# The modulation sums of a two-layer backbone move from SBUF to a PSUM bank, its background loads are issued ahead of the stores, and its buffers move down by 32 bytes

## The chip, the cores and the metric

The kernel runs on one core of a Trainium2 chip. The metric is the device time of one execution in microseconds (us), the median of several runs. Everything is float32 in memory. In the text PE is the matrix engine (TensorE), DVE the vector engine, ACT the scalar engine, POOL the GpSimd engine and SP the engine that issues most of the DMAs.

## The reference, cut to what matters

The program has two layers over 1024 tokens of width 1024, with 256 context tokens. Layer 1 is windowed attention with 16 query heads, 4 key/value heads, head size 128, a sink logit and rotary positions. Layer 2 is a gated convolution block. Each layer is modulated by a vector made from `c`:

```python
for i in range(DEPTH):
    shift, scale, gate = jnp.split((silu_c @ ada_w[i] + ada_b[i])[:, None, :], 3, axis=-1)
    h_lat = modulate(rmsnorm(x, norm_g[i]), shift, scale)        # h * (1 + scale) + shift
    ...
    if kind == 0:
        y, y_ctx = attention_layer(h_lat, h_ctx, attn_w_in[j], attn_sink[j], attn_w_out[j], cos, sin, ctx_out)
    else:
        y = conformer_conv_branch(h_lat, conv_w_in[j], conv_b_in[j], conv_dw_w[j], ..., conv_w_out[j])
    x = x + gate * y
return rmsnorm(x, final_g)
```

In the attention, 128 queries of a head meet 256 context keys and up to 384 neighbours in one softmax (`sink_softmax`), and the output is multiplied by a gate path before `attn_w_out`.

## The kernel before, in words

**Products.** Each float32 product is made of three matmuls on a rounded part and a rest: hi x hi, hi x lo, lo x hi (`mm3`). A matrix is split by ACT, which writes the rounded part, and by a subtraction `split_lo` on DVE or POOL, which writes the rest. Weights of the projections are streamed by `WStream`: `load` fetches a chunk of 1024 x 128 numbers into a page (`wraw_page`), `split` makes `whi_page` on ACT and `wlo_page` on DVE or POOL.

**Memory.** One pool of 45 pages of 4 KB per partition and one of 6 half pages hold nearly all data. `alloc` takes the page that was freed longest ago, so a load into a page waits for the last reader that this page had. Smaller named tiles (`ctile`) lie in front of the pages, among them `ident`, `vt` and `sel` in this order. PSUM has the tiles `pss` (two of two banks), `psg` (two banks) and `pso` (the banks `o0` and `o1`, which `ps_o()` takes in turn).

**Stages.** Of the span, the first 100 us load inputs, make the first modulation and project keys, values and the first queries. From 100 to about 858 us runs the attention: 128 steps, one for each head and block of 128 queries. A step emits scores (`pss<-kh_page,qh_page` and its like), then `FILL` = 12 groups of background projection matmuls (`psg<-hh_page,whi_page`), then the transposes of the probabilities (`pss<-ident,p_page`), and after each fourth step the product with the values (`pv`, into a `pso` tile, evacuated by DVE as `oz_half<-pso,zs_page`). Beside PE, DVE makes the masked scores and their sum (`p_page<-pss,mask_page,nsink`, the sum in `sc`), ACT the exponentials, POOL the scaling `p_page<-p_page,sc`; ACT and DVE split the transposed probabilities into `pthi` and `ptlo`. At each fourth head (three times) a regroup projects the next key and value heads, emits `pv` and the first scores of the new group, and then turns the value block with four transposes in `vt_split` (`pso<-ident,vf_half`). From 858 to 1047 us follows the output projection, to 1500 us the input projection and convolution of layer 2, and then its norm and output projection.

**Background work of the attention.** Two generators are advanced by the steps. `ada_rest` makes the modulation that is still missing, the gate of layer 1 and all of layer 2: 16 groups of 256 columns, each the sum over 8 row blocks of `ada_w` (loaded in turn into the tiles `dww_raw` and `wsum_raw`) times the vector `cs`. The sum is kept in the last 256 columns of `mask_page` (`acc_a`): one `tensor_scalar`, two additions of the bias over `ident`, seven `scalar_tensor_tensor` (stt). One step later PE sums over the partitions with `ones`. `low_parts` prepares the rests of both output weights, 32 items of 512 KB: load into a `low_page`, ACT rounds a half (`lhi_half`), POOL subtracts, and the page is stored to `wolA` or `wolC` in DRAM. An item takes three steps; after heads 3, 7, 11 and 15 have passed their first `LOWS` = 5 steps, no new one is begun.

**Order.** PE's instructions keep the order of the program (`pin("P")`). The order on the other engines is set by a scheduler that works on estimated times. Each engine then runs its own list strictly in order, so an instruction that waits holds all behind it; this goes for SP too, where a load whose page is not free or a store whose data is not ready holds every later DMA.

Of the kernel before, what the change touches and what calls it, by code (L numbers as in the profile page):

```python
# [9 lines left out]
F32 = mybir.dt.float32  # L10
F32R = mybir.dt.float32r
AF = mybir.ActivationFunctionType
ALU = mybir.AluOpType
# [81 lines left out]
def backbone_kernel(  # L95
# [32 lines left out]
    def ps_o(i=None):  # L128
        if i is None:
            oflip[0] ^= 1  # L130
            i = oflip[0]
        return ps.tile([P, 512], F32, tag=f"o{i}", name=nm("pso"), bufs=1)
# [10 lines left out]
    def ctile(shape, dt, name):  # L143
        return cpool.tile(shape, dt, tag=name, name=name, bufs=1)
# [13 lines left out]
    def split_lo(eng, lo, full, hi):  # L158
        return tt(eng, lo, full, hi.bitcast(F32), ALU.subtract)

    ident = ctile([P, P], F32, "ident")
    vt = ctile([P, P], F32, "vt")
    sel = ctile([P, 2], F32, "sel")
    sink = ctile([P, NH], F32, "sink")
    nsink = ctile([P, NH], F32, "nsink")
    ones = ctile([P, P], F32, "ones")
# [34 lines left out]
    class WStream:  # L201
# [19 lines left out]
        def split(self, between=None):  # L221
            if self.ns >= self.nl:
                return
            i = self.ns
            r = self.raw.pop(i)
            h, l = pg.alloc(F32R, [KT, P], "whi"), pg.alloc(F32R, [KT, P], "wlo")
            if self.hp:
                with tc.high_priority():
                    act(h, r, AF.Copy)
                    split_lo(self.lo_eng(i), l, r, h)  # L230
            else:
                act(h, r, AF.Copy)
                if between:
                    between()
                split_lo(self.lo_eng(i), l, r, h)
            pg.free(r)
            self.hl[i] = (h, l)
            self.ns += 1
# [269 lines left out]
    for pr in range(NPR):  # L508
# [35 lines left out]
        if pr == 2:  # L544
# [2 lines left out]
            SY.dma_start(out=cos, in_=k_cos)  # L547
            SY.dma_start(out=sin, in_=k_sin)

    def vt_split(vf, n, dh, dl):  # L550

        tp = ps_o()
        for i in range(n // P):
            PE.transpose(tp[:, i * P:(i + 1) * P], vf[:, i * P:(i + 1) * P], ident)
        t3 = tp[:, 0:n].rearrange("p (a b) -> p a b", b=P)
        act(dh, t3, AF.Copy)
        split_lo(V, dl, t3, dh)
# [24 lines left out]
    def ada_rest():  # L582
        todo = [(l, c0) for l, c0 in [(0, 2048 + 256 * i) for i in range(4)] + [(1, 256 * i) for i in range(12)]]
        todo = [(l, c0, kt) for l, c0 in todo for kt in range(KT)]

        def load(i):
            l, c0, kt = todo[i]
            SY.dma_start(out=ada_raw[i % 2], in_=ada_w[l, kt * P:(kt + 1) * P, c0:c0 + 256])

        load(0)  # L590
        for i, (l, c0, kt) in enumerate(todo):
            if i + 1 < len(todo):
                load(i + 1)
            raw = ada_raw[i % 2]
            if kt == 0:
                after(V.tensor_scalar(out=acc_a, in0=raw, scalar1=cs[:, kt:kt + 1], scalar2=None, op0=ALU.mult))
                for b in range(2):
                    col = (c0 - 2048 if l == 0 else 1024 + c0) // P + b
                    bs = slice(b * P, b * P + P)
                    stt(acc_a[:, bs], ident, abt[:, col:col + 1], acc_a[:, bs], ALU.mult, ALU.add)  # L600
            else:
                after(stt(acc_a, raw, cs[:, kt:kt + 1], acc_a, ALU.mult, ALU.add))
            yield
            if kt < KT - 1:
                continue
            yield
            o = ps_o()
            if c0 >= 2048:
                PE.matmul(o[0:1, 0:256], ones[:, 0:1], acc_a, start=True, stop=True)
                V.tensor_copy(acc_a[0:1], o[0:1, 0:256])  # L610
                SY.dma_start(out=gd[l][:, c0 - 2048:c0 - 1792], in_=acc_a[0:1])
            else:
                for b in range(2):
                    PE.matmul(o[:, b:b + 1], acc_a[:, b * P:b * P + P], ones[:, 0:1], start=True, stop=True)
                V.tensor_copy(mod1[:, c0 // P:c0 // P + 2], o[:, 0:2])
# [9 lines left out]
    def pair_rows(ap, m, kk):  # L625

        return ap[kk * 256:kk * 256 + 256, m * 512:m * 512 + 512].rearrange("(a p) n -> p a n", p=P)

    def low_parts():

        items = [(pair_rows(w, m, kk), d[m, kk]) for w, d in ((Wo, wolA), (Wp, wolC)) for m in range(2) for kk in range(NK)]
        for src, dst in items:
            raw = pg.alloc(F32, [2, 512], "low")
            SY.dma_start(out=raw, in_=src)
            yield "open"
            for b in range(2):
                hi = hp.alloc(F32R, None, "lhi")
                act(hi[:, 0:512], raw[:, b], AF.Copy)
                after(split_lo(G, raw[:, b], raw[:, b], hi[:, 0:512]), anchor_p)
                hp.free(hi)  # L640
                if b == 0:
                    yield "open"
            SY.dma_start(out=dst, in_=raw)
            pg.free(raw)
            yield "shut"

# [313 lines left out]
    def enqueue(key):  # L962
        fillq.append((key, job(key)))
# [58 lines left out]
    def pv(h, half):  # L1022
        g = h // 4
        c, vh, vl = kvt[g][2:5]
        o = ps_o()
        q0 = half * 4
        work = [(*(c[:, n, i * P:i * P + P] for n in (2, 3)), slice(13 + 4 * i, 17 + 4 * i), slice(0, 512)) for i in range(2)]
        for kb in range(max(q0 - 1, 0), min(q0 + 4, TB - 1) + 1):
            qa, qz = max(kb - 1, q0), min(kb + 1, q0 + 3)
            b0 = 1 + 4 * (1 - (kb - qa)) + (qa - q0)  # L1030
            n = qz - qa + 1
            if n == 1 and kb > qa:
                work.append((vh[:, kb], vl[:, kb], slice(0, 5, 4), slice(256, 512)))
            elif n == 1:
                work.append((vh[:, kb], vl[:, kb], slice(9, 22, 12), slice(0, 256)))
            else:
                work.append((vh[:, kb], vl[:, kb], slice(b0, b0 + 5 * (n - 1) + 1, 5),
                             slice((qa - q0) * P, (qz - q0 + 1) * P)))
        for n, (a, b, ps_, os_) in enumerate(work):
            last = n == len(work) - 1  # L1040
            PE.matmul(o[:, os_], a, pthi[:, ps_], start=n == 0, stop=False)
            PE.matmul(o[:, os_], a, ptlo[:, ps_], start=False, stop=False)
            PE.matmul(o[:, os_], b, pthi[:, ps_], start=False, stop=last)
        sl = slice(half * 512, half * 512 + 512)
        oz = hp.alloc(F32, None, "oz")
        stt(oz[:, 0:512], o, 0.5, zt[h][:, sl], ALU.mult, ALU.mult)
        SY.dma_start(out=ozd[h, :, sl], in_=oz[:, 0:512])
        hp.free(oz)
        if half:
            pg.free(zt.pop(h))  # L1050
            pg.free(*qt.pop(h))
# [49 lines left out]
    lows = low_parts()  # L1101
    lstate = ["shut"]
    pvq = deque()
    enqueue(("z", 0))
    enqueue(("q", 1))
    fill(18)
# [4 lines left out]
    for i, (h, qb) in enumerate(steps):  # L1111
        if qb == 0:
            for n in (() if h % 4 == 3 else (h + 1,) if h % 4 or not h else (h, h + 1)):
                enqueue(("z", n))
                if n + 1 < NH:
                    enqueue(("q", n + 1))
        if (h, qb) == (NH - 1, EARLY_FROM - 2):
            run(lows)
        if h == NH - 1 and EARLY_FROM - 2 <= qb < EARLY_FROM:
            next(projA)  # L1120
        if (h, qb) == (NH - 1, EARLY_FROM):
            next(projA)
            fillq.append((("wo", 0), early_proj()))
        if lstate[0] == "open" or h and (h % 4 < 3 or qb < LOWS):
            lstate[0] = next(lows, "shut")
        nxt = steps[i + 1] if i + 1 < len(steps) else None
        regroup = nxt and nxt[1] == 0 and nxt[0] % 4 == 0
        if nxt and nxt[1] == 0:
            fill(1000, ("q", h + 1))
        if nxt and not regroup:  # L1130
            scores(*nxt)
        if not regroup:
            fill(15 if h and h % 4 == 0 and qb < 4 else FILL)
        if pvq:
            pv(*pvq.popleft())
        if regroup:
            g = nxt[0] // 4
            old = kvt[g - 1]
            run(job(("k", g)))
            transposes(h, qb)  # L1140
            run(job(("v", g)))
            pv(h, 1)
            pg.free(*old)
            scores(*nxt)
            vlate.pop(g)()
            continue
        transposes(h, qb)
        if qb % 4 == 3:
            pvq.append((h, qb // 4))
        for _ in range(2 if qb == 1 or qb == 6 and h % 2 else 1):  # L1150
            next(adag, None)
# [575 lines left out]
```

## Time and the profile before

| | before |
|---|---|
| runs | 1756.67, 1757.55, 1760.27 us |
| median | 1757.55 us |
| span of the profiled execution | 1752.9 us |
| PE busy / DVE / ACT / POOL | 98% / 66% / 51% / 51% |

For the profiled execution the span is known, not its own device time; the median of the runs stands 4.65 us above this span. A prediction of the time is made as the change of the span, added to the median. A row of a timeline gives the start, the duration, the engine, the operation with output and inputs, and in brackets how long the engine had been idle before it and what ended this idle time.

### The profile page before, as it was taken

What the parts mean: (1) busy time and instruction counts of PE and PEld (TensorE: products, weight loads), DVE (VectorE), ACT (ScalarE), POOL (GpSimd) and SP (SyncE); (2) the same over time, 40 slices, a digit from 0 to 9 for tenths busy, and PEclk for the clock granted to TensorE, in tenths of its full rate; (3) what the DMA queues carried; (4) which work ended last, traced back from release to release, by engine and by line L of the source; (5) the groups of instructions that cost most, each with busy time, mean ns of one, the idle gap of its engine ahead of it and who ended that gap; (6) DMA issues with size and microseconds to landing.
All of it is one profiled execution on the core that took longest, in us unless ns stands there. A gap on an engine that the chain in (4) does not pass through costs nothing.

```text
span 1752.9 us, 23877 instructions
## 1 busy us (share of the span) xinstructions
PE 1720.7 (98%) x8420; PEld 1424.8 (81%) x8420; DVE 1148.3 (66%) x2079; ACT 889.4 (51%) x1548; POOL 895.4 (51%) x705
## 2 busy tenths in 40 slices
PE   7999999999999999999999999999999999999997
PEld 4788888888888888888888888888888888788886
DVE  6755564556546563656315189999999999867823
ACT  7555553445345444545334355554665564466731
POOL 0245654566636565653101267998898888130300
PEclk9999999999999999999999999999999999999999
DMA  9334443444334542436777733011121202377971
GB/s 313 107 82 139 136 133 85 145 147 145 100 105 143 152 142 87 136 119 203 279 250 239 241 90 105 13 54 31 43 79 36 91 30 79 120 254 243 325 264 48
DMA packets 195324, 242.45 MB, mean 138 GB/s; under 512 B 11798, under 2 KB 126790, under 8 KB 195204
## 3 DMA queue, kind: packets, MB, share of 16 engines
q1 hardware_dynamic: 188516, 230.10, 40.3%
q10 hardware_dynamic: 6688, 10.83, 2.6%
q8 instruction: 66, 1.08, 0.3%
q14 instruction: 54, 0.44, 0.1%
HBM read 188.70 MB, written 41.69 MB: 131 GB/s over the span
## 4 chain that ended last, share of the span: by engine, by line
PE 86%; DMA 5%; DVE 3%; POOL 2%; ACT 2%; issue 2%; SPq 1%; ACTq 0%; POOLq 0%; DVEq 0%
PE psg L89 44%; PE pss L89 22%; PE pso L89 19%; DMA araw_page<-in_ada_w_dram 1%; POOL rope_half L89 1%; DMA low_page<-in_conv_w_out_dram 1%; DMA rope_half<-rope_half 1%; SPq L89 1%; DMA low_page<-in_attn_w_out_dram 1%; DMA wolC<-low_page 1%; DVE mask_page L89 1%; ACT p_page L89 0%; POOL wlo_page L89 0%; POOL low_page L89 0%; DMA wraw_page<-in_attn_w_in_dram 0%
## 5 line engine op out<-in xcount | busy, mean ns | idle before, releaser
L89 POOL TENSOR_TENSOR odd_half<-odd_half,prod_half 128x513 f32<-128x513 f32 (+2 forms) x252 | 312.8, 1250 | 24.2 <-ACT prod_half L89 11.0
L89 PE MATMUL psg<-hh_page,whi_page 128*128 128x512 f32 x600 | 237.6, 396 | 0.0
L89 PE MATMUL psg<-hh_page,wlo_page 128*128 128x512 f32 x600 | 236.9, 395 | 0.0
L89 PE MATMUL psg<-hl_page,whi_page 128*128 128x512 f32 x600 | 236.8, 395 | 0.0
L89 POOL TENSOR_TENSOR wlo_page<-wraw_page,whi_page 128x1024 fp32r<-128x1024 f32 x70 | 173.1, 2475 | 104.1 <-ACT whi_page L89 83.2
L89 ACT ACTIVATE prod_half<-ubuf,dww 128x513 f32<-128x513 f32 (+2 forms) x252 | 165.1, 674 | 107.3 <-POOL odd_half L89 105.1
L89 POOL TENSOR_SCALAR p_page<-p_page,sc 128x640 f32<-128x640 f32 (+1 forms) x128 | 100.8, 787 | 224.4 <-DVE sc L89 208.7
L89 PE MATMUL psg<-h2h_page,whi_page 128*128 128x512 f32 x464 | 183.9, 396 | 0.0
L89 PE MATMUL psg<-h2h_page,wlo_page 128*128 128x512 f32 x464 | 183.0, 394 | 0.0
L89 PE MATMUL psg<-h2l_page,whi_page 128*128 128x512 f32 x464 | 182.4, 393 | 0.0
L89 DVE SCALAR_TENSOR_TENSOR pss<-ubuf,dww,pss 128x512 f32<-128x512 f32 (+3 forms) x270 | 172.3, 670 | 0.1
L89 DVE SCALAR_TENSOR_TENSOR pss<-ubuf,wsum,pss 128x512 f32<-128x512 f32 (+3 forms) x270 | 171.7, 670 | 0.2
L89 DVE TENSOR_TENSOR ptlo<-pss,pthi 128x640 fp32r<-128x640 f32 (+1 forms) x144 | 103.3, 717 | 64.0 <-ACT pthi L89 62.8
L89 ACT ACTIVATE p_page<-p_page,sc 128x641 f32<-128x641 f32 (+1 forms) x128 | 102.7, 802 | 74.1 <-DVE sc L89 69.7
L89 ACT ACTIVATE pthi<-pss 128x640 fp32r<-128x640 f32 (+1 forms) x144 | 88.6, 615 | 91.7 <-PE pss L89 86.3
L89 PEld LDWEIGHTS psg<-hh_page,wlo_page 128*128 128x128 f32 x600 | 112.9, 188 | 26.3
L89 PEld LDWEIGHTS psg<-hh_page,whi_page 128*128 128x128 f32 x600 | 113.0, 188 | 20.8 <-DVE kvc_page L89 0.2
L89 PEld LDWEIGHTS psg<-hl_page,whi_page 128*128 128x128 f32 x600 | 112.9, 188 | 20.7
L89 ACT ACTIVATE whi_page<-wraw_page 128x1024 fp32r<-128x1024 f32 x88 | 92.6, 1053 | 69.0 <-PE psg L89 25.5
L89 PE MATMUL pso<-h2l_page,whi_page 128*128 128x512 f32 x304 | 119.9, 394 | 0.0
L89 PE MATMUL pso<-h2h_page,whi_page 128*128 128x512 f32 x304 | 119.8, 394 | 0.0
L89 PE MATMUL pso<-h2h_page,wlo_page 128*128 128x512 f32 x304 | 119.6, 394 | 0.0
(244 smaller groups left out, 4105.2 us busy)
## 6 DMA issues: line engine op xcount, KB each, us to landing
wraw_page<-in_conv_w_in_dram SPq DMA_DIRECT2D x48, 512.0 KB
wraw_page<-in_attn_w_in_dram SPq DMA_DIRECT2D x40, 512.0 KB
wol_page<-wolA SPq DMA_DIRECT2D x32, 512.0 KB
wo_page<-in_attn_w_out_dram SPq DMA_DIRECT2D x32, 512.0 KB
wo_page<-in_conv_w_out_dram SPq DMA_DIRECT2D x32, 512.0 KB
wol_page<-wolC SPq DMA_DIRECT2D x32, 512.0 KB
rope_half<-rope_half ACTq DMA_DIRECT2D x80, 128.0 KB
araw_page<-in_ada_w_dram SPq DMA_DIRECT2D x32, 256.0 KB
```

The lines of the kernel that those rows point to most:

```text
L89: r = f(*a, **k)
```

## The change

Five edits are made together.

1. The tile `sel` is dropped and its two columns become columns 112 and 113 of `vt`. Every tile and page behind it starts 32 bytes lower: before at 32 beyond a multiple of 64, now at a multiple of 64. `ident` and `vt` stay where they were.
2. Where POOL makes a `wlo_page`, it does so in two halves of 128 x 512 instead of one operation of 128 x 1024.
3. `ada_rest` keeps its sum in the left half of the PSUM bank `o1` for the whole attention. Sixteen copies of 128 x 256 from PSUM to `acc_a` are added, one step after the last product of a group; PE's sum over the partitions goes into the right half of the same bank.
4. As `o1` is taken, `pv` and `vt_split` use bank `o0` only during the attention.
5. The store of a low item is written behind the load of the next one, and its page is freed that much later. Where a step begins no item, the outstanding store is written at once.

```diff
-    sel = ctile([P, 2], F32, "sel")
+    sel = vt[:, 112:114]
 ...
-                split_lo(self.lo_eng(i), l, r, h)
+                if self.lo_eng(i) is G:
+                    for a in range(0, KT, KT // 2):
+                        split_lo(G, *(t[:, a:a + KT // 2] for t in (l, r, h)))
+                else:
+                    split_lo(self.lo_eng(i), l, r, h)
 ...
+    vbank = []
     def vt_split(vf, n, dh, dl):
-        tp = ps_o()
+        tp = ps_o(*vbank)
 ...
         load(0)
+        bank = ps_o(1)
+        acc, o = bank[:, 0:256], bank[:, 256:512]
 ...
-                after(V.tensor_scalar(out=acc_a, in0=raw, scalar1=cs[:, kt:kt + 1], scalar2=None, op0=ALU.mult))
+                after(V.tensor_scalar(out=acc, in0=raw, scalar1=cs[:, kt:kt + 1], scalar2=None, op0=ALU.mult))
 ...
-                    stt(acc_a[:, bs], ident, abt[:, col:col + 1], acc_a[:, bs], ALU.mult, ALU.add)
+                    stt(acc[:, bs], ident, abt[:, col:col + 1], acc[:, bs], ALU.mult, ALU.add)
             else:
-                after(stt(acc_a, raw, cs[:, kt:kt + 1], acc_a, ALU.mult, ALU.add))
+                after(stt(acc, raw, cs[:, kt:kt + 1], acc, ALU.mult, ALU.add))
             yield
             if kt < KT - 1:
                 continue
+            V.tensor_copy(acc_a, acc)
             yield
-            o = ps_o()
 ...
+    made = []
+    def store():
+        while made:
+            dst, raw = made.pop()
+            SY.dma_start(out=dst, in_=raw)
+            pg.free(raw)
     def low_parts():
         for src, dst in items:
             raw = pg.alloc(F32, [2, 512], "low")
             SY.dma_start(out=raw, in_=src)
+            store()
             yield "open"
 ...
-            SY.dma_start(out=dst, in_=raw)
-            pg.free(raw)
+            made.append((dst, raw))
             yield "shut"
+        store()
 ...
     def pv(h, half):
-        o = ps_o()
+        o = ps_o(0)
 ...
+    vbank.append(0)
     enqueue(("z", 0))
 ...
         if lstate[0] == "open" or h and (h % 4 < 3 or qb < LOWS):
             lstate[0] = next(lows, "shut")
+        else:
+            store()
```

PE's order is the same as before. The first place where another engine's order differs is on POOL, ahead of the first regroup (about 262 to 277 us of the span). Here `wlo` is the rest of a weight chunk, the two `rope` rows with the same number form the rotated query, and `ql` is its rest. Before:

```order
99 L89 TENSOR_TENSOR ql_page_2391<-rope_half_2480,qh_page_2390 128x512
100 L89 TENSOR_SCALAR p_page_2536<-p_page_2536,sc_2537 128x640
101 L89 TENSOR_TENSOR wlo_page_2643<-wraw_page_2277,whi_page_2642 128x1024
102 L89 TENSOR_SCALAR p_page_2578<-p_page_2578,sc_2579 128x512
103 L89 TENSOR_TENSOR wlo_page_2947<-wraw_page_2646,whi_page_2946 128x1024
104 L89 TENSOR_TENSOR rope_half_2592<-rope_half_2592,sin_page_664 128x512
105 L89 TENSOR_TENSOR rope_half_2593<-rope_half_2593,rope_half_2592 128x512
106 L89 TENSOR_TENSOR rope_half_2649<-rope_half_2649,sin_page_664 128x512
107 L89 TENSOR_TENSOR ql_page_2391<-rope_half_2593,qh_page_2390 128x512
```

After:

```order
99 L89 TENSOR_TENSOR ql_page_2398<-rope_half_2487,qh_page_2397 128x512
100 L89 TENSOR_SCALAR p_page_2545<-p_page_2545,sc_2546 128x640
101 L89 TENSOR_TENSOR wlo_page_2651<-wraw_page_2284,whi_page_2650 128x512 x2
102 L89 TENSOR_SCALAR p_page_2586<-p_page_2586,sc_2587 128x512
103 L89 TENSOR_TENSOR rope_half_2600<-rope_half_2600,sin_page_663 128x512
104 L89 TENSOR_TENSOR wlo_page_2957<-wraw_page_2655,whi_page_2956 128x512 x2
105 L89 TENSOR_TENSOR rope_half_2601<-rope_half_2601,rope_half_2600 128x512
106 L89 TENSOR_TENSOR rope_half_2658<-rope_half_2658,sin_page_663 128x512
107 L89 TENSOR_TENSOR ql_page_2398<-rope_half_2601,qh_page_2397 128x512
```

The first rope operation of this chunk has moved ahead of the second `wlo`, and each `wlo` is two operations.

The second place is on SP at about 577 to 584 us, where a low page is stored and two are loaded. Before:

```order
229 L89 DMA dww_raw<-in_ada_w_dram 128x256
230 L89 DMA wolC<-low_page_5506 128x1024
231 L89 DMA ozd<-oz_half_5607 128x512
232 L89 DMA low_page_5672<-in_conv_w_out_dram 128x2x512
233 L89 DMA wsum_raw<-in_ada_w_dram 128x256
234 L89 DMA low_page_5823<-in_conv_w_out_dram 128x2x512
```

After:

```order
229 L89 DMA dww_raw<-in_ada_w_dram 128x256
230 L89 DMA wolC<-low_page_5529 128x1024
231 L89 DMA ozd<-oz_half_5631 128x512
232 L89 DMA low_page_5696<-in_conv_w_out_dram 128x2x512
233 L89 DMA low_page_5847<-in_conv_w_out_dram 128x2x512
234 L89 DMA wsum_raw<-in_ada_w_dram 128x256
```

The store (`wolC<-low_page`) stands ahead of both loads in both kernels; only the second load has passed one load of `ada_w`.

The third place is on DVE at the end of the first stage, where the first group of `ada_rest` begins (`hf`, `hh`, `hl` are the modulated input and its parts, `abt` the bias). Before, it stands at about 68 us of the span:

```order
77 L89 COPY abt<-pso_679 128x32
78 L89 TENSOR_SCALAR mask_page_739<-dww_raw,cs 128x256
79 L89 TENSOR_SCALAR dwb_8289<-vt 128x16
80 L89 SCALAR_TENSOR_TENSOR mask_page_739<-ident,abt,mask_page_739 128x128 x2
81 L89 SCALAR_TENSOR_TENSOR mask_page_739<-wsum_raw,cs,mask_page_739 128x256
82 L89 TENSOR_SCALAR hf_page_687<-psg_682,mod_183 128x512
```

After, it stands where before it the span had reached about 98 us:

```order
105 L89 TENSOR_TENSOR rope_page_768<-rope_page_768,rope_half_767 128x512
106 L89 TENSOR_SCALAR pso_1052<-dww_raw,cs 128x256
107 L89 TENSOR_TENSOR wlo_page_960<-wraw_page_823,whi_page_959 128x1024
108 L89 SCALAR_TENSOR_TENSOR pso_1052<-ident,abt,pso_1052 128x128
109 L89 TENSOR_TENSOR ql_page_755<-rope_page_768,qh_page_754 128x512
110 L89 SCALAR_TENSOR_TENSOR pso_1052<-ident,abt,pso_1052 128x128
111 L89 SCALAR_TENSOR_TENSOR pso_1052<-wsum_raw,cs,pso_1052 128x256
```

The whole group has moved behind the modulation of the first stage and now stands around the split of a weight chunk (`wlo_page`) and of the first query (`ql_page`).

More of the change, by code (lines that the diff above doesn't have):

```diff
@@ L605, in ada_rest @@
                 continue
+            V.tensor_copy(acc_a, acc)
             yield
-            o = ps_o()
             if c0 >= 2048:
-                PE.matmul(o[0:1, 0:256], ones[:, 0:1], acc_a, start=True, stop=True)
-                V.tensor_copy(acc_a[0:1], o[0:1, 0:256])
+                PE.matmul(o[0:1], ones[:, 0:1], acc_a, start=True, stop=True)
+                V.tensor_copy(acc_a[0:1], o[0:1])
                 SY.dma_start(out=gd[l][:, c0 - 2048:c0 - 1792], in_=acc_a[0:1])
```

## The prediction

> **What bounds the kernel now.** I read the page first, then the windows by stage, then PE's waits inside the attention, and last the timelines of the places that these waits name. Two rows of the page say who is busy:
>
> ```profile
> span 1752.9 us, 23877 instructions
> PE 1720.7 (98%) x8420; PEld 1424.8 (81%) x8420; DVE 1148.3 (66%) x2079; ACT 889.4 (51%) x1548; POOL 895.4 (51%) x705
> ```
>
> PE is the bound, and no edit changes its list. All edits but the lower addresses act between about 70 and 860 us. In the windows, whose columns are the stretch, its length, the busy time of PE, PEld, DVE, ACT and POOL, the granted clock, the DMA share and GB/s, the attention reads:
>
> ```profile
> 100.00:858.00 758.00, 751.28 (x4142) 647.96 (x4141) 423.52 (x832) 368.21 (x774) 410.91 (x347) 1.00 0.44 136
> ```
>
> PE idles 758.00 - 751.28 = 6.7 us there. This is the most that the edits to background work can bring, 0.4% of the span. The waits of PE between 130 and 860 us name nearly all of it (total us, times, longest):
>
> ```profile
> PE pss L89 <- DVE ptlo L89: 3.6, 2, 3.2
> PE pss L89 <- DVE sc L89: 1.3, 3, 0.9
> PE psg L89 <- DVE rope_half L89: 1.0, 1, 1.0
> PE pss L89 <- POOL p_page L89: 0.5, 1, 0.5
> ```
>
> Their sum is 6.4 us, and three single waits of 3.2, 1.0 and 0.9 us make 5.1 of it. So the question is which of these three the edits take away, and what they put in their place.
>
> **The sums in PSUM.** The rows of DVE by form show what the sums cost now, and what an operation of the same form with its sum in PSUM costs (the convolution's row):
>
> ```profile
> L89 DVE SCALAR_TENSOR_TENSOR mask_page<-wsum_raw,cs,mask_page 128x256 f32<-128x256 f32 x61 | 48.6, 797 | 0.0
> L89 DVE SCALAR_TENSOR_TENSOR mask_page<-dww_raw,cs,mask_page 128x256 f32<-128x256 f32 x45 | 36.4, 810 | 3.0 <-DMA dww_raw<-in_ada_w_dram 2.9
> L89 DVE SCALAR_TENSOR_TENSOR mask_page<-ident,abt,mask_page 128x128 f32<-128x128 f32 x30 | 16.8, 600 | 0.1
> L89 DVE SCALAR_TENSOR_TENSOR pss<-ubuf,dww,pss 128x256 f32<-128x256 f32 x15 | 7.2, 481 | 0.1
> L89 DVE SCALAR_TENSOR_TENSOR mask_page<-wsum_raw,cs,mask_page x64: 468/484/2203, 68.8 to 824.6; 128x256 f32<-128x256 f32 x64
> L89 DVE COPY mask_page<-pso x8: 393/410/416, 141.4 to 826.2; 1x256 f32<-1x256 f32 x8
> ```
>
> The fifth row, of one tile, gives minimum, median and maximum: half of the sums take 484 ns, some over 2 us. The operation on PSUM takes 481 ns. So the gain lies in the stretched ones alone: 61 x 0.316 + 45 x 0.329 = 34 us of DVE, and up to 30 x 0.36 = 11 us for those of `ident`, if they fall to half of a 128x256. Against that stand 16 copies of about 0.41 us (the last row, on one partition, is the nearest), 6.6 us. DVE is relieved by some 35 us in 758, but it is busy 424 of them, so nearly all of this turns into idle DVE. What counts is where a stretched sum stands ahead of an operation that PE waits for. The timeline shows one:
>
> ```profile
> 351.34 1.29 POOL L89 TENSOR_TENSOR low_page<-low_page,lhi_half 128x512 f32<-128x512 f32 x1
> 351.64 1.27 DVE L89 SCALAR_TENSOR_TENSOR mask_page<-dww_raw,cs,mask_page 128x256 f32<-128x256 f32 x1
> 352.84 0.87 DVE L89 CUSTOM_DVE_ANT_0 p_page<-pss,mask_page,nsink 128x640 f32<-128x640 f32 x1
> 353.77 0.44 PE L89 MATMUL pss<-kh_page,qh_page 128*128 128x384 f32 x1 [0.94 <-DVE sc L89]
> ```
>
> The sum ends with POOL's subtraction, 0.94 us of PE's idle time follow. At 0.48 us the softmax operation behind it starts 0.79 us sooner: **-0.8 us**. The copies are placed among these sums, one step ahead of PE's use of them, and a step lasts 758 / 128 = 5.9 us; they cost nothing unless one stands ahead of a softmax operation as this sum did, and then at most 0.41 us.
>
> **POOL's halves and the rope.** POOL's rows, and its largest wait in the attention:
>
> ```profile
> L89 POOL TENSOR_TENSOR low_page<-low_page,lhi_half 128x512 f32<-128x512 f32 x64 | 83.7, 1307 | 0.0
> L89 POOL TENSOR_TENSOR wlo_page<-wraw_page,whi_page 128x1024 fp32r<-128x1024 f32 x34 | 82.8, 2436 | 31.8 <-ACT whi_page L89 29.3 <-PE psg L89 1.5 <-POOL p_page L89 1.0
> POOL p_page L89 <- DVE sc L89: 208.7, 90, 13.5
> ```
>
> Two halves at 1.307 cost 2.61 against 2.44 us, so 34 x 0.178 = 6 us more POOL work, under 209 us in which POOL waits for the softmax. Under this cover it costs nothing; where a split stands ahead of an operation that PE waits for, 0.18 us. The order brings more. The rows of the one wait for `rope_half`:
>
> ```profile
> 262.41 0.47 ACTq L89 DMA_DIRECT2D rope_half<-rope_half  x1
> 268.88 2.41 POOL L89 TENSOR_TENSOR wlo_page<-wraw_page,whi_page 128x1024 fp32r<-128x1024 f32 x1 [4.37 <-ACT whi_page L89]
> 271.25 1.48 POOL L89 TENSOR_TENSOR rope_half<-rope_half,sin_page 128x512 f32<-128x512 f32 x1
> 272.80 1.29 POOL L89 TENSOR_TENSOR rope_half<-rope_half,rope_half 128x512 f32<-128x512 f32 x1
> 274.06 1.30 POOL L89 TENSOR_TENSOR rope_half<-rope_half,sin_page 128x512 f32<-128x512 f32 x1
> 275.30 1.31 POOL L89 TENSOR_TENSOR ql_page<-rope_half,qh_page 128x512 fp32r<-128x512 f32 x1
> 276.65 0.69 DVE L89 TENSOR_TENSOR rope_half<-psg,cos_page 128x512 f32<-128x512 f32 x1 [4.48 <-POOL ql_page L89]
> 277.40 0.39 PE L89 MATMUL psg<-hch_page,whi_page 128*128 128x256 f32 x1 [0.99 <-DVE rope_half L89]
> ```
>
> Five POOL operations stand in a chain behind the 4.37 us in which POOL waited for a weight chunk. After, the first rope operation stands ahead of that chunk. Its data was sent at 262.4, so it fits into the idle stretch, and the chain is shorter by 1.48 - 0.17 = 1.3 us, more than the 0.99 that PE waits: **-1.0 us**.
>
> **Loads ahead of stores.** The longest wait, in the timeline:
>
> ```profile
> 580.29 1.29 POOL L89 TENSOR_TENSOR low_page<-low_page,lhi_half 128x512 f32<-128x512 f32 x1
> 581.61 0.33 SPq L89 DMA_DIRECT2D wolC<-low_page  x1
> 581.98 0.42 SPq L89 DMA_DIRECT2D ozd<-oz_half  x1
> 582.46 0.78 SPq L89 DMA_DIRECT2D low_page<-in_conv_w_out_dram  x1
> 588.64 1.15 ACT L89 ACTIVATE lhi_half<-low_page 128x512 fp32r<-128x512 f32 x2 [5.95 <-DMA low_page<-in_conv_w_out_dram]
> 591.29 0.44 PE L89 MATMUL pss<-kh_page,qh_page 128*128 128x384 f32 x1 [3.19 <-DVE ptlo L89]
> ```
>
> SP holds the load until POOL's subtraction has ended and the store is out; ACT then waits 5.95 us for it with the probabilities queued behind, and PE 3.19. By its words the edit is aimed at just this. But in the order after, the store still stands ahead of both loads here, and ACT's rounding must still wait; elsewhere the scheduler had most loads ahead of their stores already. I put **0** on it; it is between -3.2 (the load goes early) and, since a page is held one item longer and FIFO pages then reach a later reader, +3.2 for each load that becomes so late elsewhere.
>
> **One bank for the values.** At a regroup the four transposes of the value block no longer have a bank of their own:
>
> ```profile
> 295.91 0.69 DVE L89 SCALAR_TENSOR_TENSOR oz_half<-pso,zs_page 128x512 f32<-128x512 f32 x1 [6.33 <-PE pso L89]
> 296.41 0.60 PE L89 MATMUL pso<-ident,vf_half 128*128 128x128 f32 x4
> ```
>
> They must now wait until DVE has read the bank at 296.60: 0.2 us, with the first softmax and score work of the group queued behind on PE. Three regroups: **+0.6 us**. Other `pv` products are some 20 us apart and find the bank free.
>
> [...]
>
> **The first group.** Its four DVE operations leave 68 us, where 1.3 us of them stood ahead of the next `hf_page`, and come back around 98 us. PE's waits near the old place are for other things, so I take 0, between -0.5 and +0.5.
>
> **Lower addresses.** The trace has all PE operands at 32 beyond a multiple of 64, so none of it shows a matmul at the new place. It bounds what a fixed toll for each matmul could be. These are the first of 15 matmuls of 512 columns in a row, the first of 23 steps of 256, and the last of these:
>
> ```profile
> 269.51 0.40 PE L89 MATMUL psg<-hh_page,whi_page 128*128 128x512 f32 x1
> 273.00 0.28 PE L89 MATMUL psg<-hch_page,whi_page 128*128 128x256 f32 x1
> 275.69 0.29 PE L89 MATMUL psg<-hch_page,wlo_page 128*128 128x256 f32 x1
> ```
>
> One takes 3.49 / 15 = 0.2327 us, the other 2.69 / 23 = 0.1170. Twice the short one is 1.3 ns more than the long one, so a toll is at most about that, and 8,420 x 1.3 ns = 11 us is the outer bound of the gain. As this is the size of rounding, I take 0. [...]
>
> **The sum.** Besides, 6.4 - 3.2 - 0.94 - 0.99 = 1.3 us of small waits remain; with a less loaded DVE and a reordered ACT they go from -1.3 to +0.3, and I take -0.3. Together -0.8 - 1.0 + 0 + 0.6 - 0.3 = -1.5 us on the span of 1752.9. The median stands 4.65 us above the span, which I leave as it is: 1757.55 - 1.5 = **1756.0 us**. This case's own range is -3.1 (all small waits gone, no toll at the banks) to +0.7 (only the rope gained, the rest against me): 1754.4 to 1758.3.
>
> **The rivals.** *The late load goes too.* The wait of 3.2 us hangs on when POOL ends its subtraction; with fewer collisions with DVE and the halves, POOL may be done some us sooner, or the swapped rows may help. For it speaks that POOL's chain is tight there; against it, the unchanged order. It gives -1.5 - 3.2 = -4.7, 1752.8 us, and at the most all 6.7 us, 1750.8.
>
> *A page comes late.* One low page more is held, and the 45 pages are given out in the order of their freeing. A load whose page is not yet free stops SP, with the `ada_w` loads, the weight chunks and the output stores queued behind, and ACT then stops ahead of the probabilities, as at 582 us. The price is 3.2 us a place. One place turns -1.5 into +1.7, which is no measurable loss; from two places on, +4.9 or 1762.5 us, it is slower. For it speaks that it happened once already with the pages of before; against it, that SP's order is almost unchanged.
>
> *The addresses matter.* Up to 11 us by the bound above; a third of it, with the sum, gives -5, 1752.5 us; all of it, 1745.
>
> *The change does little of what it says.* The loads are put ahead in the text but hardly in SP's list; this is in the forecast already.
>
> **How the numbers follow.** I give the forecast 0.32, the late load 0.30, the late page 0.28 and the addresses 0.10. A difference under 0.2%, 3.5 us, can hardly be told from none for this kernel. The late load (-4.7) and the addresses count as faster: 0.40. The forecast counts as same, and 0.04 of the late page with it (one place): 0.36. The other 0.24 of the late page are slower. For 8 in 10 the range reaches down to 1748, which leaves out half of the addresses' case, and up to 1763, just past two late places, which leaves out perhaps 0.1 with more of them.
>
> **What would show it.** In the profile after: sums on `pso` at about 0.48 us with no long ones; no PE wait for `rope_half` near 276 us; none of 0.9 us for `sc` near 352; the wait near 587 still about 3 us; about 0.2 us for `oz` at each regroup; the pitch of matmuls unchanged at 0.2327 us. PE's waits between 130 and 860 us would sum to about 5 us instead of 6.4. I am wrong if PE's pitch moves, if a wait for `ptlo` behind a load stands at new places, or if PE's idle time outside the attention changes by over 1 us.

## The result and the profile after

The changed kernel takes 1754.7 us in the median of 12 runs (1751.7 to 1757.6), the kernel before 1757.3 us in 12 runs beside it (1754.1 to 1760.5). The ratio is 0.9990, with a 95% interval of 0.9983 to 0.9998: a gain of 2.6 us between the medians, of 1.8 us by the ratio, 0.3 to 3 us by the interval. The forecast was 1756.0, a gain of 1.5 us. The experiments below show that the sum was nearly right for a wrong reason, so by luck.

The profiled execution of the changed kernel is not one of its quicker ones. Its span is longer than that of before, though the median of the runs is shorter, so single places are read from it and not the total. In every run of the record the device time stands 1.8 us above the span of the same execution. The 4.65 us that the prediction added to the span of before are these 1.8 us and 2.9 us by which that execution was quicker than the median.

```profile
span 1754.5 us, 23940 instructions
PE 1721.4 (98%) x8420; PEld 1424.8 (81%) x8420; DVE 1108.6 (63%) x2095; ACT 891.5 (51%) x1548; POOL 896.1 (51%) x741
```

The windows of the attention and of one stretch in it (stretch, length, busy time of PE, PEld, DVE, ACT and POOL, granted clock, DMA share, GB/s) show 40 us less DVE work and no more PE work than before, and one stretch in which the granted clock is not 1.00:

```profile
100.00:858.00 758.00, 750.81 (x4129) 647.18 (x4129) 383.28 (x849) 369.21 (x774) 411.32 (x375) 1.00 0.43 136
580.00:600.00 20.00, 16.19 (x77) 13.76 (x76) 8.78 (x22) 8.74 (x18) 8.27 (x8) 0.83 0.49 136
```

PE's waits between 130 and 860 us after (total, times, longest):

```profile
PE pss L89 <- DVE ptlo L89: 4.1, 2, 3.8
PE pso L89 <- DVE mask_page L89: 1.6, 1, 1.6
PE psg L89 <- DVE rope_half L89: 0.7, 1, 0.7
PE pso L89 <- ACT lhi_half L89: 0.3, 2, 0.2
PE pso L89 <- DVE oz_half L89: 0.2, 1, 0.2
```

Before, these waits summed to 6.4 us; now to 6.9. The waits for `sc` and `p_page` are gone and that for `rope_half` is shorter, but the wait behind the late load has grown and a new one for `mask_page` has come. PE's list is the same in both kernels, so its 8,420 matmuls can be set side by side: from 100 to 300 us the two executions are within 0.7 us of each other; at 400 us the changed kernel is 2.5 us ahead, at 600 us 0.8 behind, at 858 us 2.5 behind, and from there to the end this difference falls by 1 us. What the four edits to the background work visibly give and take lies between 200 and 860 us.

**The sums.** DVE's rows by form, of the attention:

```profile
L89 DVE SCALAR_TENSOR_TENSOR pso<-wsum_raw,cs,pso 128x256 f32<-128x256 f32 x61 | 29.4, 481 | 0.0
L89 DVE SCALAR_TENSOR_TENSOR pso<-ident,abt,pso 128x128 f32<-128x128 f32 x30 | 10.6, 353 | 0.5
L89 DVE COPY mask_page<-pso 128x256 f32<-128x256 f32 x16 | 6.8, 422 | 0.1
```

The stretched sums are gone (481 ns mean, 797 before). At the place that the prediction had picked, the sum runs its 0.48 us beside POOL's subtraction, and PE's wait of 0.94 us has gone:

```profile
348.85 1.30 POOL L89 TENSOR_TENSOR low_page<-low_page,lhi_half 128x512 f32<-128x512 f32 x1
350.04 0.48 DVE L89 SCALAR_TENSOR_TENSOR pso<-dww_raw,cs,pso 128x256 f32<-128x256 f32 x1
350.43 0.88 DVE L89 CUSTOM_DVE_ANT_0 p_page<-pss,mask_page,nsink 128x640 f32<-128x640 f32 x1
```

Matmul by matmul, PE gains 1.19 us here, and 0.4 to 0.7 us each near 226, 374, 395, 547 and 722 us, together 3.7 us.

**The rope.** POOL's timeline ahead of the first regroup:

```profile
268.04 1.29 POOL L89 TENSOR_TENSOR rope_half<-rope_half,sin_page 128x512 f32<-128x512 f32 x1 [3.88 <-DMA rope_half<-rope_half]
269.29 2.54 POOL L89 TENSOR_TENSOR wlo_page<-wraw_page,whi_page 128x512 fp32r<-128x512 f32 x2
274.70 1.29 POOL L89 TENSOR_TENSOR ql_page<-rope_half,qh_page 128x512 fp32r<-128x512 f32 x1
```

The rope operation does stand ahead of the chunk, but it waits for its own transfer until 268.04 and so pushes the chunk back; PE's wait falls from 0.99 to 0.7 us only.

**The late load and the clock.** The timeline at the longest wait:

```profile
579.68 0.33 SPq L89 DMA_DIRECT2D wolC<-low_page  x1
580.06 0.42 SPq L89 DMA_DIRECT2D ozd<-oz_half  x1
580.53 2.17 SPq L89 DMA_DIRECT2D low_page<-in_conv_w_out_dram  x2
587.23 1.15 ACT L89 ACTIVATE lhi_half<-low_page 128x512 fp32r<-128x512 f32 x2 [6.40 <-DMA low_page<-in_conv_w_out_dram]
589.88 0.69 PE L89 MATMUL pss<-kh_page,qh_page 128*128 128x384 f32 x1 [3.81 <-DVE ptlo L89]
592.07 0.63 PE L89 MATMUL psg<-hl_page,whi_page 128*128 128x512 f32 x1
592.50 0.63 PE L89 MATMUL psg<-hh_page,wlo_page 128*128 128x512 f32 x1
```

The store is still first. In SP's list the two loads now follow each other, and the first takes 6.7 us to ACT's start, against 6.2 before. The second goes out 1.8 us behind the first, before it was 1.6, so it is not a closer second load that makes the difference. PE stands for 3.81 us, and then its matmuls of 512 columns start 0.43 us apart instead of 0.232, for about 5 us: the granted clock has dropped to half (0.50 from 589 to 594 us). Beside the kernel before this place costs 0.6 us for the wait and 2.2 for the slow matmuls.

**The new wait.** DVE and PE near 826 us:

```profile
826.10 1.22 DVE L89 TENSOR_TENSOR ozl_page<-ozf_page,ozh_page 128x1024 fp32r<-128x1024 f32 x1
827.23 0.41 DVE L89 COPY mask_page<-pso 128x256 f32<-128x256 f32 x1
827.70 0.59 PE L89 MATMUL pso<-mask_page,ones 128*1 128x256 f32 x2 [1.65 <-DVE mask_page L89]
```

The sixteenth copy stands behind a split for the output projection, and PE, which needs the sum, is already there. Before, with no copy between, PE had the finished sum at this place at once. It costs 1.5 us.

### The profile page after: what moved, and what is told of

The parts are those of the page before. It is cut to its first block, busy times and chain, and to the rows that moved or that the text cites. A ratio compares the mean times of both kernels' runs of the same rounds, so it can differ in the third digit from the quotient of the medians.

```text
span 1754.5 us, 23940 instructions
## 1 busy us (share of the span) xinstructions
PE 1721.4 (98%) x8420; PEld 1424.8 (81%) x8420; DVE 1108.6 (63%) x2095; ACT 891.5 (51%) x1548; POOL 896.1 (51%) x741
## 4 chain that ended last, share of the span: by engine, by line
PE 87%; DMA 6%; DVE 2%; POOL 2%; ACT 2%; issue 1%; SPq 1%; ACTq 0%; DVEq 0%; POOLq 0%
PE psg L89 45%; PE pss L89 22%; PE pso L89 19%; DMA araw_page<-in_ada_w_dram 1%; DMA low_page<-in_conv_w_out_dram 1%; DMA rope_half<-rope_half 1%; POOL rope_half L89 1%; SPq L89 1%; DMA x_page<-in_x_dram 1%; DMA low_page<-in_attn_w_out_dram 0%; DMA wolC<-low_page 0%; DMA wraw_page<-in_attn_w_in_dram 0%; POOL low_page L89 0%; ACT lhi_half L89 0%; DVE ptlo L89 0%
## 5 line engine op out<-in xcount | busy, mean ns | idle before, releaser
L89 POOL TENSOR_TENSOR wlo_page<-wraw_page,whi_page 128x512 fp32r<-128x512 f32 (+1 forms) x106 | 178.7, 1702 | 96.9 <-ACT whi_page L89 67.6
```

What stands on the lines that cost most here:

```text
L89: r = f(*a, **k)
```

## The experiments

Each kernel was timed in rounds against the kernel before. First the change was taken apart, and four of its edits were made alone; the single bank came with the sums.

**The sums alone.** Edit: `bank = ps_o(1)`, the sums, the copies, `ps_o(0)` in `pv` and `vt_split`, as in the diff.

> The kernel before with only the sums in the PSUM bank (and the value products kept in the other bank). Theory A (stretched sums ahead of the softmax operations, and a rope operation that moves ahead of a weight chunk): all sums at about 0.48 us, PE's waits near 226, 277, 353, 374, 395 and 722 us get shorter as in the trace after, together some 3 to 4 us; the transposes at the three regroups wait 0.3 us more each; a new wait of 1.5 us near 826 us behind the copy. Net -1 to -3 us, ratio 0.9985 to 0.9995. Rival B (the gain comes from the addresses): no change, ratio 0.9995 to 1.0005. Rival C (the gain comes from the order of loads and stores): no change here.

Measured 1.0004 (0.9994 to 1.0014): no gain, so theory A's net falls. The waits ahead of the softmax did get shorter, but the new wait was there, and in this execution the clock fell behind it. The first two of its waits, and the window around the place:

```profile
PE pso L89 <- DVE mask_page L89: 1.8, 1, 1.8
PE pss L89 <- DVE ptlo L89: 1.7, 2, 1.5
820.00:840.00 20.00, 17.70 (x90) 14.66 (x89) 11.76 (x21) 14.06 (x24) 3.51 (x5) 0.91 0.94 342
```

Between 800 and 858 us of the kernel before, this execution loses 4.4 us. What the sums win they give back there.

**POOL's halves alone.**

```diff
-                split_lo(self.lo_eng(i), l, r, h)
+                if self.lo_eng(i) is G:
+                    for a in range(0, KT, KT // 2):
+                        split_lo(G, *(t[:, a:a + KT // 2] for t in (l, r, h)))
```

> The kernel before with only POOL's weight split in two halves. Theory A: POOL has 6 us more work under idle time; the rope operation ahead of the first regroup stands between the halves, which shortens that chain by 1.2 us at most, so PE's wait near 277 us falls from 0.99 to 0 or a few tenths. Net 0 to -1 us, ratio 0.9994 to 1.0. If the halves were the main part of the gain, the ratio would be 0.9985 like the whole change.

Measured 0.9991 (0.9983 to 1.0000). PE's wait for `rope_half` was still 1.0 us, so the reason given for a gain is not it; whether there is a gain, and from what, stays open.

**The addresses alone.**

```diff
-    sel = ctile([P, 2], F32, "sel")
+    sel = vt[:, 112:114]
```

> The kernel before with only the two columns folded into the other tile, so that all pages lie 32 bytes lower; the order of all engines is the same as before. Theory A: no change, ratio 0.9996 to 1.0004, the pitch of matmuls 0.232 us, weight loads from DRAM no shorter. Rival B: some of the gain is here, ratio 0.9985 to 0.9992, with shorter transfers in the first 60 us or a lower pitch.

Measured 0.9989 (0.9981 to 0.9998): as much as the whole change, with the order of every engine as before. My theory had no place for this.

**The store behind the load, alone.** Edit: `made`, `store()` and its three calls, as in the diff.

> The kernel before with only the store of a low item behind the next load. Theory A: at the place near 582 us the store still stands ahead, and the two loads now follow each other at once and share the transfer, so the wait near 587 us is as long or longer, 3.2 to 4 us; if it passes the length after which the granted clock falls, as in the trace after, some 2 us more follow at half speed. Net 0 to +3 us, ratio 1.0 to 1.0015. Rival C (the edit does what it says): that wait is gone, -3 us, ratio 0.998.

Measured 0.9998 (0.9989 to 1.0008). The load took 6.2 us as before, the wait at 589 us was 2.9 us, not 3.2 to 4, and was followed by ten matmuls of 512 columns at half speed. Alone the edit brings nothing that can be measured, and the rival that it does what it says falls.

Next came the question whether the gain of the addresses is real. The same order of all engines was run with the pages at three other places; only the padding of the small tile differs:

```diff
-    sel = ctile([P, 2], F32, "sel")
+    sel = ctile([P, 16], F32, "sel")[:, 0:2]      # 24 for 64 bytes higher, 32 for 96
```

> The kernel before with the small tile padded so that all pages lie 32 bytes higher: at multiples of 64 bytes again, but at other places than in the change. The order of all engines is that of before. Rival B (multiples of 64 bytes are worth 1 to 2 us): ratio 0.9985 to 0.9993, as with the addresses of the change alone (0.9989). Theory A (addresses do nothing, that result was scatter): 0.9997 to 1.0003.

> The same with all pages 64 bytes higher, so again 32 beyond a multiple of 64. Rival B: 0.9997 to 1.0003, like the kernel before. Theory A: the same. A ratio near 0.999 here would say that the scatter between programs is as large as the effect that is looked for.

> The same with all pages 96 bytes higher, at multiples of 64 again. Rival B: ratio 0.9985 to 0.9993. Theory A: 0.9997 to 1.0003.

> The changed kernel with the small tile put back, so that all pages lie where they lay before; the other four edits stay and all engines keep the order of the changed kernel. Theory A (the gain is the sums' and the reordering's): ratio to the kernel before 0.9985 to 0.9993 as for the whole change. Rival B (the gain is the addresses'): 0.9997 to 1.0005.

| pages | kernel | ratio to before | 95% interval |
|---|---|---|---|
| 32 lower, multiples of 64 | addresses alone | 0.9989 | 0.9981 to 0.9998 |
| 32 higher, multiples of 64 | up32 | 0.9993 | 0.9983 to 1.0002 |
| 96 higher, multiples of 64 | up96 | 0.9988 | 0.9980 to 0.9997 |
| 64 higher, 32 beyond | up64 | 1.0001 | 0.9992 to 1.0010 |
| as before, 32 beyond | the changed kernel without this edit | 1.0001 | 0.9992 to 1.0010 |

This puts the gain of the change on the addresses, and on the multiple of 64 rather than on the place. The other four edits together are worth nothing that these runs can tell (1.0001). The evidence is the pattern, not one pair: the effect is of the size of the intervals, all four kernels at multiples of 64 lie at 0.9988 to 0.9993, and of the five others, the three edits alone among them, four lie at 0.9998 to 1.0004. The fifth, POOL's halves alone, has 0.9991 at the old addresses, so a changed order may move the time as far. At the same mean granted clock the difference stays: with 0.997, up32 and up96 took 1753.7 us in the mean of ten runs, the kernel before beside them 1755.2 in fourteen. The pages and the small tiles behind `sel` moved together; which of them counts was not tested.

What the addresses act on was asked next. The profiled executions of six kernels at 32 beyond and six at multiples of 64 (two are those below) were compared. The pitch of 512-column matmuls is 231.5 to 231.7 ns in both groups, and between 858 and 1500 us, where PE hardly waits, the times agree within 0.6 us. In the kernels that keep the order of before, the busy time of DVE, ACT and POOL is within 0.4% of it. But the 2048-byte packets of transfers between 100 and 860 us take 108.8 to 110.8 ns in the mean of the first six kernels and 105.8 to 108.8 in the second, and the 1024-byte packets of the first 60 us 51.0 to 51.8 against 49.7 to 50.8. The two ranges of the first kind touch, and the 1024- and 4096-byte packets between 100 and 860 us show no such split. This hints at the transfers and no more. So two kernels held loads alone, with pages at either place:

> Loads alone, no computing: in turn 80 loads of 512 KB in packets of 512 bytes, 80 in 1024, 64 in 2048 and 64 in 4096, from the kernel's own weights into 40 pages that lie 32 beyond a multiple of 64 bytes; then the pages are stored. It computes nothing of the reference. If the addresses act on the transfers, this kernel is 1 to 3% slower than its twin, most of it in the packets of 512 and 1024 bytes; if they act elsewhere, the two agree within 0.3%.

> The twin with the same loads and stores and the pages 32 bytes higher, at multiples of 64 (not of 256). If the addresses act on the transfers, 1 to 3% faster than the other; else the same within 0.3%.

They took 500.76 us (500.68 to 500.77) and 500.94 us (500.79 to 501.41), so the aligned one is not faster. The windows of the first, here without busy engines (stretch, length, POOL's busy time, clock, DMA share, GB/s), show why this test is a weak one: the queues are full throughout (a DMA share of 0.99 to 1.18 in its five stretches of 100 us).

```profile
100.00:200.00 100.00, 0.00 (x0) 1.00 1.15 321
300.00:400.00 100.00, 0.00 (x0) 1.00 1.04 398
```

This stream of loads is not faster at multiples of 64, though its 1024-byte packets took 51.1 ns against 51.6. Whether a single load lands sooner while the engines work in the same memory, which is what PE's waits hang on, is not shown. One row bears on it: the late load near 582 us took 5.66, 5.95 and 6.08 us to ACT's start in the three kernels at multiples of 64 that keep the order of before, and 6.18 and 6.54 us in the two at 32 beyond (before, up64); but 6.70 us in the changed kernel and 6.57 with its old addresses. The mechanism stays open.

The last two kernels were aimed at the waits. In the first, each store is tied behind the next load in SP's list, as the edit meant it:

```diff
-            SY.dma_start(out=raw, in_=src)
-            store()
+            store(SY.dma_start(out=raw, in_=src))
 ...
+            if behind is not None:
+                tc.add_manual_dep(st.ins, behind.ins.name, mybir.DependencyInfo(
+                    mybir.DependencyClass.NoSync, mybir.DependencyReason.DATA), reason="behind the load")
```

> The changed kernel with each store of a low item tied behind the next load in SP's list, as the edit's text has it: this moves the store in two places, ahead of 438 us and at 580 us. Theory: PE's waits for the split probabilities near 438 and 587 us (0.5 and 3.8 us in the trace after, and two more of half speed behind the second) come from the load that stands behind the store. Then they fall to under 1 us together and the ratio to the kernel before to 0.9965 to 0.998. Rival: the load waits for its page all the same (it is freed by the product of gate and value output), or shares the transfer with the next load, and the ratio stays at 0.9985 to 0.9993.

Measured 0.9980 (0.9971 to 0.9989), 1751.3 us, at the edge of what the theory asked for. The interval overlaps that of the change (0.9983 to 0.9998), so the times alone do not part the two; the trace does at this place. The timeline where the late load was:

```profile
577.82 0.33 SPq L89 DMA_DIRECT2D ozd<-oz_half  x1
578.20 0.43 SPq L89 DMA_DIRECT2D low_page<-in_conv_w_out_dram  x1
578.72 0.44 SPq L89 DMA_DIRECT2D wolC<-low_page  x1
583.20 1.15 ACT L89 ACTIVATE lhi_half<-low_page 128x512 fp32r<-128x512 f32 x2 [2.77 <-DMA low_page<-in_conv_w_out_dram]
```

The load goes out 2.3 us sooner, as soon as the evacuation of the value product, the last to use its page, is done (577.79 us), and ACT starts on it 5.0 us later instead of 6.7. The second load goes out only 6.3 us behind it. The kernel after this one has the same two numbers, and in the other ten traces, where the second load follows within 1.5 to 2.9 us, the first takes 5.7 to 6.7 us. That the two loads share the transfer there is an estimate from these times. No two matmuls between 560 and 610 us start more than 0.29 us apart: the wait is gone. The wait at 826 us remains, and with it the half clock. PE's timeline there:

```profile
822.25 0.59 PE L89 MATMUL pso<-mask_page,ones 128*1 128x256 f32 x2 [1.76 <-DVE mask_page L89]
824.09 0.63 PE L89 MATMUL psg<-woh_page,ozh_page 128*128 128x512 f32 x1
824.52 0.63 PE L89 MATMUL psg<-wol_page,ozh_page 128*128 128x512 f32 x1
826.93 0.39 PE L89 MATMUL psg<-wol_page,ozh_page 128*128 128x512 f32 x1
827.16 0.39 PE L89 MATMUL psg<-woh_page,ozl_page 128*128 128x512 f32 x1
```

The second leaves out the sums in PSUM and the single bank, and keeps the rest.

> The last kernel without the sums in PSUM and without the single bank that goes with them: lower addresses, POOL's halves and the load tied ahead of the store. The sums alone measured 1.0004 (0.9994 to 1.0014). If they are worth nothing or cost (0.3 us at each of three regroups, 1.5 us near 826 us), this kernel is as fast as the last or faster, 0.996 to 0.998 of before; if they bring the 3 to 4 us of shorter waits that the traces show, it is slower than the last by 1 us or more.

Measured 0.9967 (0.9954 to 0.9979), 1749.7 us in 5 runs, 1.6 us under the last one. The two intervals overlap, but the traces agree with it: without the sums the wait near 826 us, 1.8 us in the last kernel, is gone, and no wait over 0.8 us is left. The attention's window and the longest waits:

```profile
100.00:858.00 758.00, 754.82 (x4154) 649.86 (x4153) 412.91 (x830) 367.99 (x775) 417.53 (x383) 1.00 0.44 137
PE pss L89 <- DVE ptlo L89: 0.8, 2, 0.5
PE pss L89 <- DVE sc L89: 0.8, 1, 0.8
PE psg L89 <- DVE rope_half L89: 0.5, 1, 0.5
```

PE idles 3.2 us in the attention instead of 6.7. This is the fastest version found: it is about 5.5 us faster than the kernel before, and its interval lies below that of the change.

## Why the prediction was right or wrong

The sign, the range and nearly the size were right, but by luck: the prediction put -1.5 us on the four edits to the background work and 0 on the addresses, and the runs show about 0 (1.0001) and about -2 us. Two steps failed, and their errors cancelled. Of its own signs, the sums at 0.48 us, the pitch and the wait near 352 us came out; the wait for `rope_half` (0.7 us, not none) and the sum of PE's waits (6.9 us, not about 5) did not. The upper end of its narrow range, +0.7, does not follow from the terms shown: -1.0 + 0.6 + 0.3, and 0.5 for the first group, give +0.4, and +0.8 with a copy of 0.41 us in the way.

**Lower addresses: wrong.** The term was 0, with a bound of 11 us from PE's pitch. It measured about 2 us. (Not quite all of PE's operands lay at 32 beyond: `ident`, which the transposes read, stayed at a multiple of 64.) The step looked for a toll at PE, and at PE the runs show none, as it said: 512-column matmuls start 231.5 to 231.7 ns apart at both places. It had no row for transfers at the other place, and it should have left that term open downward by more than rounding. The rival *the addresses matter* had a chance of 0.10 and is what happened, though with a smaller amount than a third of its bound. Nor do the runs make a start at a multiple of 256 bytes the cause: at 32 lower 26 of the 45 pages have one, at 96 higher only 6, at 32 higher 4, and all three measured a gain of like size (0.9989, 0.9988 and 0.9993).

**The sums in PSUM: right in size, wrong in the end.** DVE fell by 40 us (35 were taken, the terms add up to 38), the sums to 481 ns, and the wait near 352 us went with 1.2 us (0.8 expected). The small waits gave more than the 0.3 us that were taken, some 2.5. The step that failed is *the copies cost nothing*: I bounded one by its own 0.41 us ahead of a softmax operation and missed that PE itself waits for it. At the last group it stands behind a split of 1.22 us, and PE waits 1.65 us.

**The rope: mis-sized.** The order moved as shown, but I took its data to have landed by the time POOL was idle. It landed at 268.04, and -1.0 us became -0.3.

**The load ahead of the store: right to put no gain on it.** The order after told truly that the store stays first. The place got dearer in the profiled execution, by 0.6 us for the wait and by 2.2 us for the clock. Why the load took 0.5 us longer is open; the same load differs by as much between kernels of one order (5.7 to 6.5 us). The rival of the late page named the mechanism of this wait; it came at the old place and, but for 0.3 us for `ptlo` at 438 us, not at new ones.

**One bank: right.** The transposes start 0.32 us later at each regroup (0.2 expected), in the timeline behind the read that ends at 296.02. The bracket names ACT's rounding, which ends close by; at the second regroup the trace names the read itself:

```profile
295.33 0.69 DVE L89 SCALAR_TENSOR_TENSOR oz_half<-pso,zs_page 128x512 f32<-128x512 f32 x1 [6.38 <-PE pso L89]
296.16 0.63 PE L89 MATMUL pso<-ident,vf_half 128*128 128x128 f32 x4 [0.16 <-ACT lhi_half L89]
```

**The first group: nothing to be seen.** The term was 0. At 100 us the two executions are 0.2 us apart, and within the first 100 us they differ by up to 1.3 us, so more cannot be said.

**The clock: missing.** No step priced what follows a wait. The traces record when the granted clock is half: for 3.4 us at a time, in two of them (after, and the store behind the load alone) for 6.8 us, and a part of this lies under the wait itself: after, the half clock lasts from 588.1 to 594.9 us, and PE waits until 589.88. In the twelve traces, PE's matmul starts lie 2.0 us or more apart at 12 places between 100 and 860 us. Behind eight of these gaps, of 2.0 to 4.1 us, the clock falls; behind four, of 2.0, 2.3, 3.2 and 3.5 us (the last in the kernel before), it does not, nor behind the five of 1.7 to 1.9 us. So the length of a gap alone does not part the two, as the clock falls behind one of 2.0 us and not behind one of 3.5; what decides it is not shown. Whole runs show the price: beside up32, up64 and up96 the kernel before took 1755.2 us in the mean of 14 runs with a mean granted clock of 0.997, and 1758.3 in the eight with 0.995 or less.

## What to carry to other kernels

With PE 98% busy, as here, a wait cost its own time and in some places what the clock took behind it: near 590 us, after, a wait of 3.8 us and 2.2 us of slow matmuls. In the attention of these traces no gap under 2.0 us was followed by a fall of the clock, so one wait of 3 us could cost more here than several short ones of the same sum. Ask of every added step who needs its result, not only what it holds up: the copy took 0.4 us where it stood and kept PE waiting for 1.65. An edit that puts a load ahead of a store does so only if the scheduler's list shows it; tied in that list, it took PE's wait of 3.8 us away. Before a term is put at nothing, measure it alone: here the addresses, put at 0, brought the gain, and the edits that the sum was built on brought none together.

## What was not expected of the hardware

With its pages at multiples of 64 bytes this kernel was about 0.1% faster than with pages 32 beyond (0.9988 to 0.9993 in three kernels, 1.0001 in two controls), while the pitch of the matmuls (231.5 to 231.7 ns) and the time of a pure stream of loads (500.76 and 500.94 us) did not change. PE's clock was found at half speed behind a gap of 2.0 us (near 822 us with the load tied ahead), where 512-column matmuls started 0.43 us apart, and at full speed behind one of 3.5 us (near 591 us in the kernel before).
